# Tiles of a hybrid attention and FFN layer placed at other addresses: the operands of FFN1's up products 64 bytes past their split weights modulo 512, the query, key-value and gate weights 352 bytes further

## The chip, the cores and the metric

The kernel runs on one core of a Trainium2 chip. The metric is the time of one execution in microseconds of device time, the median of several runs. A profiled execution leaves a trace of every instruction on the engines: TensorE (PE, with its weight loads shown apart as PEld), VectorE (DVE), ScalarE (ACT), GpSimd (POOL), and the DMA queue that SyncE (SP) feeds.

## What is computed

One layer over 512 latent tokens and 256 context tokens of width 1024, all in float32: a half-step SwiGLU FFN, token mixing (latent attention with eight heads beside a chunked spatial gate), and a second half-step FFN on the latent tokens.

```python
x = ffn_sublayer(x, mx[0], mx[1], mx[2], norm1_w, ffn1_w1, ffn1_w3, ffn1_w2)
ctx = ffn_sublayer(ctx, mc[0], mc[1], mc[2], norm1_w, ffn1_w1, ffn1_w3, ffn1_w2)
proj = modulate(rms_norm(x, norm2_w), mx[3], mx[4]) @ w_in
...
x = x + mx[5] * token_mix(proj, k_all, v_all, rope, ...)
x = ffn_sublayer(x, mx[6], mx[7], mx[8], norm3_w, ffn2_w1, ffn2_w3, ffn2_w2)
```

with `ffn_sublayer(h) = h + 0.5 * gate * ((silu(n @ w1) * (n @ w3)) @ w2)`, `n` the normed and modulated input. FFN1 works on all 768 tokens, FFN2 on the 512 latent ones; the hidden width is 2816, in 22 blocks of 128.

## The kernel before

Tokens lie along the free dimension, features along the 128 partitions. Every product is made of three matmuls (`mm3`, L165): each operand is kept as a high part in float32r and a low part (the rest), and high by high, low by high and high by low are added up in PSUM. In a name of a matmul the first operand is the moving one, the second the weights: `mm<-hl,oph` streams `hl` past the weights `oph`.

```python
nc.tensor.matmul(out, lh, rh, start=first, stop=False, skip_group_check=more)
nc.tensor.matmul(out, lh, rl, start=False, stop=False, skip_group_check=more)
nc.tensor.matmul(out, ll, rh, start=False, stop=last, skip_group_check=more)
```

Weights come from HBM by SyncE's queue into `raw` or `block` tiles; ScalarE rounds 512 columns to the high part (`oph`) and VectorE subtracts for the low part (`opl`). Five such pairs rotate (`OPS`).

The stages in the order of time:

- First pass of FFN1, to about 61 us: norm and modulation make `hh` and `hl` (L239, L240; 8 blocks of 768 tokens); the first two blocks of the hidden width are done here, with latent tokens 512 wide (`step_mm`) and context tokens 256 wide (`first_ctx`, L573 to L582). The weights of the last three k are split into tiles of the starting pool (`op5` to `op7`).
- FFN1 proper, to about 487 us: two more blocks of the hidden width by plain products, then one level of Winograd's scheme for the up products. Its blocks are four quarters of `hh` and `hl` (L1020) and the token differences `u2`, `u3`, `u4` (L1023), each 384 wide; between them stand down products, whose moving operands `gh`, `gl` are read 256 wide. The order is written out by hand and kept (`Flow`, `Winograd`).
- The last down chunk, 384 wide, to about 538 us. Some of its weights are split into tiles that have come free: `cbl`, `block_l`, `s_l`.
- The input projection (`in_k`, L1292) reads `hh` and `hl` 384 and 256 wide past `oph` and, for the rotary keys, past `kpw` (64 columns). The u and v projection (`uv_unit`, L1364) turns it round: `hh` is the weights, `oph` streams 512 wide. The queries (`q_tile`, L1460) stream `wqh` (L1325) past `cqh` (L1322); the keys and values (`k_mm`, L1526) stream `wkvh` past `ckvh`; the gate (`gate`, L1575) streams `vnh`, which is `mixh` (L1312), past `wsuh`.
- Attention, the output projection (`mixh` past `oph` and `uo`, then `uo` only), and FFN2 (blocks `b11` to `b22`, `t1` to `t4`, 256 wide; `gh`, 512 wide).

Tiles are placed by pools on two stacks, one from the left end of SBUF and one from the right. A pool on the right ends where the one before it begins, so a larger tile under it moves all that come later towards lower addresses. Some small tiles that nobody reads are there only to shift others: `pad_left`, `pad_right` (L237), `pad_mix`, `pad_oap`, `pad_hap` (L1890), `pad_w`, `pad_f2`.

The address of a tile in its partition, modulo 512 bytes, as the pools place it (a step of 128 columns in a weight tile, and one k or one block in a moving tile, is a multiple of 512, so the whole tile has one value):

| tile | role | before | after |
|---|---|---|---|
| `oph`, `opl`, `block_l` | split weights | 448 | 448 |
| `cbl`, `s_l` | split weights of the last down chunk | 384 | 384 |
| `hh`, `hl` | moving; weights in the u and v projection | 448 | 0 |
| `u2`, `u3`, `u4` | moving | 448 | 0 |
| `op5` to `op7` | split weights in the first pass | 448 | 0 |
| `kpw` | weights of the rotary keys, by k | 64, 320 | 128, 384 |
| `gh`, `gl` in FFN1 | moving | 384 | 384 |
| `wqh`, `wql` with `cqh`, `cql` | moving with weights | 96, 96 | 448, 448 |
| `wkvh`, `wkvl` with `ckvh`, `ckvl` | moving with weights | 96, 448 | 448, 448 |
| `mixh` (as `vnh`) with `wsuh` | moving with weights | 448 or 192, 96 | 448 or 192, 448 |
| `mixh`, `mixl` with `uo0`, `uo1` | moving with weights | 448, 384 | 448, 384 |
| `b11`, `b21`, `b22`, `t1` to `t4` (`b12`) | moving in FFN2 | 384 (448) | 384 (448) |
| `w0`, `w1` | split weights at the start of FFN2 | 320 | 320 |

Of the kernel before, what the change touches and what calls it, by code (L numbers as in the profile page):

```python
# [9 lines left out]
F32 = mybir.dt.float32  # L10
# [7 lines left out]
P = 128  # L18
# [155 lines left out]
def layer_kernel(ctx: ExitStack, tc: tile.TileContext, xT, wfirst, wst, wada, wuq, wkpe, cols, wrope, vnw, rope, out):  # L174
# [59 lines left out]

    hctx = ExitStack()
    with right():
        ctx.enter_context(tc.tile_pool(name="pad", bufs=1)).tile([P, 8], F32, name="pad_right")  # L237
        hpool = hctx.enter_context(tc.tile_pool(name="hpool", bufs=1))
    hh = hpool.tile([P, NK, 768], F32R, name="hh")  # L239
    hl = hpool.tile([P, NK, 768], F32R, name="hl")  # L240
# [1067 lines left out]
    p2 = p2ctx.enter_context(tc.tile_pool(name="p2", bufs=1))  # L1308
# [8 lines left out]
    vk = p2.tile([P, 6], F32, name="vk")  # L1317
    rk = p2.tile([P, 6], F32, name="rk")
    sv = p2.tile([P, 6], F32, name="sv")
    p1actx = ExitStack()  # L1320
    p1a = p1actx.enter_context(tc.tile_pool(name="p1a", bufs=1))
    cqh = p1a.tile([P, 2, 512], F32R, name="cqh")  # L1322
# [198 lines left out]
    with right():  # L1521
        kp = kctx.enter_context(tc.tile_pool(name="kpool", bufs=1))
    kn = kp.tile([P, 6, HEADS, QH], F32, name="kn")
    vv = kp.tile([P, 6, HEADS, P], F32R, name="vv")

    def k_mm(t, n, o):  # L1526
        s = slice(t * P, t * P + P)
        m = slice(n * 512, n * 512 + 512)
        mm3(nc, o, (ckvh[:, s], ckvl[:, s]), (wkv[0][:, m], wkv[1][:, m]), True, True)
# [353 lines left out]
    with right():  # L1883
        hap = hactx.enter_context(tc.tile_pool(name="hap", bufs=1))

    def block(pool, name):
        return tuple(pool.tile([P, 4, 256], F32R, bufs=1, name=f"{name}{p}") for p in "hl")

    B11, B21 = block(hap, "b11"), block(hap, "b21")
    hap.tile([P, 16], F32, name="pad_hap")  # L1890
    hbctx = ExitStack()
    with right():
        hbp = hbctx.enter_context(tc.tile_pool(name="hbp", bufs=1))
# [312 lines left out]
```

## Time and profile before

| what | value |
|---|---|
| median of 3 runs | 1112.83 us (1112.6 to 1113.48) |
| span of the profiled execution | 1110.9 us |
| TensorE busy | 1104.4 us, 7616 matmuls |
| weight loads busy | 1056.4 us |
| VectorE, ScalarE, GpSimd busy | 882.9, 537.7, 308.9 us |
| DMA | 125.96 MB, 113 GB/s in the mean |

The profiled execution's own time is given as its span, from the first to the last instruction; the median of the runs is 1.9 us longer, which is what lies around it. A row of the timeline has the start in us, the duration in us, the engine, the line, the operation, the names out<-in, and the shapes. Line L59 is that of a helper through which most instructions pass, so instructions are told apart by their tiles. A matmul's end in the trace is modelled, and rows overlap; the starts are recorded, and the distance from one start to the next is the pace.

### The profile page before, as it was taken

Reading aid. Unit: us, or ns where it says so; the run is one execution under the profiler, and the core shown is the slowest. Engines: PE = TensorE matmul, PEld = TensorE weight load, DVE = VectorE, ACT = ScalarE, POOL = GpSimd, SP = SyncE. Lnnn points to the kernel's source line nnn. Section 1 sums busy time; section 2 is a strip of 40 time slices with the busy share of each in tenths; the row PEclk is TensorE's granted clock in tenths of the full one; section 3 lists DMA queues with packets and bytes.
Section 4 is the critical chain, followed back from the end, with each engine's and each line's share of the span. In section 5 each row is a group of like instructions: output and inputs, shape, how many; then the busy total and the mean of one; then the engine's idle time right before and its main releaser. Section 6 shows DMA issues by size and latency. Waiting matters only on the chain.

```text
span 1110.9 us, 19724 instructions
## 1 busy us (share of the span) xinstructions
PE 1104.4 (99%) x7616; PEld 1056.4 (95%) x7616; DVE 882.9 (79%) x1590; ACT 537.7 (48%) x1110; POOL 308.9 (28%) x268
## 2 busy tenths in 40 slices
PE   9999999999999999999999999999999999999998
PEld 7899999999999999999988889999999989898997
DVE  5779898888888778866756899978886969696884
ACT  6545422431444214444755559985554536353451
POOL 0003303312243023300008427750014425152330
PEclk9999999999999999999999999999999999999999
DMA  9721353344334765312242211003221422333302
GB/s 357 272 65 50 123 169 127 114 135 151 120 107 151 239 200 190 114 59 79 86 134 94 76 38 34 26 21 114 77 96 57 144 86 83 108 115 114 114 2 95
DMA packets 35678, 125.96 MB, mean 113 GB/s; under 512 B 3712, under 2 KB 10624, under 8 KB 30976
## 3 DMA queue, kind: packets, MB, share of 16 engines
q1 hardware_dynamic: 35440, 124.63, 33.1%
q8 instruction: 60, 0.98, 0.4%
q14 instruction: 34, 0.28, 0.1%
q10 hardware_dynamic: 144, 0.06, 0.0%
HBM read 122.58 MB, written 2.10 MB: 112 GB/s over the span
## 4 chain that ended last, share of the span: by engine, by line
PE 94%; DVE 3%; DMA 1%; ACT 1%; issue 0%; POOL 0%; SPq 0%; ACTq 0%; DVEq 0%; POOLq 0%
PE mm L59 55%; PE one L59 19%; PE big L59 8%; PE mm L169 2%; PE mm L170 2%; PE mm L168 2%; PE big L596 1%; PE mm L581 1%; DMA scale<-wada 1%; PE big L170 1%; PE big L168 1%; PE big L169 1%; PE mm L330 1%; DMA x<-xT 0%; DVE opl L59 0%
## 5 line engine op out<-in xcount | busy, mean ns | idle before, releaser
L59 DVE TENSOR_TENSOR opl<-block,oph 128x512 fp32r<-128x512 f32 x216 | 190.0, 888 | 29.8 <-ACT oph L59 27.4
L59 POOL TENSOR_TENSOR block<-block 128x512 f32<-128x512 f32 x69 | 104.1, 1509 | 380.2 <-DVE opl L59 377.6
L59 ACT CAST oph<-block 128x512 fp32r<-128x512 f32 x216 | 133.9, 622 | 109.0 <-PE mm L59 81.9
L59 PE MATMUL mm<-gh,oph 128*128 128x256 f32 (+2 forms) x573 | 176.7, 308 | 0.0
L59 PE MATMUL mm<-gl,oph 128*128 128x256 f32 (+2 forms) x573 | 176.4, 308 | 0.0
L59 PE MATMUL mm<-gh,opl 128*128 128x256 f32 (+2 forms) x573 | 176.4, 308 | 0.0
L59 DVE SCALAR_TENSOR_TENSOR x<-mm,g,x 128x512 f32<-128x512 f32 (+2 forms) x136 | 79.1, 601 | 47.4 <-PE mm L59 47.1
L59 PEld LDWEIGHTS mm<-gl,oph 128*128 128x128 f32 x573 | 107.6, 188 | 5.6
L59 PEld LDWEIGHTS mm<-gh,oph 128*128 128x128 f32 x573 | 107.6, 188 | 5.5
L59 PEld LDWEIGHTS mm<-gh,opl 128*128 128x128 f32 x573 | 107.6, 188 | 5.4
L59 ACT CAST oph<-raw 128x512 fp32r<-128x512 f32 x113 | 68.7, 621 | 77.5 <-PE mm L59 53.0
L59 DVE TENSOR_TENSOR opl<-raw,oph 128x512 fp32r<-128x512 f32 x113 | 77.6, 702 | 11.6 <-ACT oph L59 10.9
L59 POOL TENSOR_TENSOR block<-s,block 128x512 f32<-128x512 f32 x35 | 46.6, 1331 | 130.4 <-DVE opl L59 129.6
L59 PE MATMUL mm<-hh,oph 128*128 128x384 f32 (+2 forms) x195 | 65.2, 334 | 0.0
L59 PE MATMUL mm<-hl,oph 128*128 128x384 f32 (+2 forms) x195 | 64.8, 333 | 0.0
L59 PE MATMUL mm<-hh,opl 128*128 128x384 f32 (+2 forms) x195 | 64.8, 332 | 0.0
L59 DVE SCALAR_TENSOR_TENSOR junk<-raw,cb 128x1024 bf16<-128x1024 f32 x48 | 62.2, 1309 | 0.0
L59 POOL TENSOR_TENSOR s<-block 128x512 f32<-128x512 f32 x34 | 55.6, 1636 | 10.6 <-DMA block<-wst 10.6
L59 DVE SCALAR_TENSOR_TENSOR raw<-raw,cb 128x1024 f32<-128x1024 f32 x32 | 42.2, 1323 | 7.9 <-DMA raw<-wada 7.9
L59 PE MATMUL one<-hl,oph 128*128 128x384 f32 x144 | 48.1, 334 | 0.0
L59 PE MATMUL one<-hh,oph 128*128 128x384 f32 x144 | 48.1, 334 | 0.0
L59 PE MATMUL one<-hh,opl 128*128 128x384 f32 x144 | 48.1, 334 | 0.0
(711 smaller groups left out, 3382.8 us busy)
## 6 DMA issues: line engine op xcount, KB each, us to landing
raw<-wst SPq DMA_DIRECT2D x77, 512.0 KB, 3.9
block<-wst SPq DMA_DIRECT2D x36, 1024.0 KB, 5.0
raw<-wada SPq DMA_DIRECT2D x56, 512.0 KB, 4.3
scale<-wada SPq DMA_DIRECT2D x16, 512.0 KB, 9.0
x<-xT SPq DMA_DIRECT2D x5, 512.0 KB, 6.3
raw<-wfirst SPq DMA_DIRECT2D x8, 256.0 KB, 9.1
out<-x SPq DMA_DIRECT2D x7, 256.0 KB, 2.3
raw<-wuq SPq DMA_DIRECT2D x2, 384.0 KB, 5.1
```

The costliest lines, as they stand in the source:

```text
L59: return lambda *a, **k: self.tc.keep_in_program_order(f(*a, **k))
L168: nc.tensor.matmul(out, lh, rh, start=first, stop=False, skip_group_check=more)
L169: nc.tensor.matmul(out, lh, rl, start=False, stop=False, skip_group_check=more)
L170: nc.tensor.matmul(out, ll, rh, start=False, stop=last, skip_group_check=more)
L330: pin(nc.tensor.matmul(pa[q, :P], scw[:, kt, 2 - 2 * w : 34 - 2 * w], units[d][w][:, kt * P : kt * P + P], start=w == 0 and kt < 4, stop=w ...
L581: pin(nc.tensor.matmul(o, l[:, c], r, start=k == 0 and m == 0 and w == 0, stop=k == NK - 1 and m == 2, skip_group_check=True))
L596: pin(nc.tensor.matmul(two(pbs[i]), ops[k][lo][:, i * P : i * P + P], lat(r, k), start=False, stop=k == NK - 1 and m == 2, skip_group_chec ...
```

## The change

Four pads: `pad_right` grows from 8 to 120 floats, a new `pad_p2` of 88 floats stands behind the small tiles of the token mixing, a new `pad_kp` of 16 floats and `pad_hap`, grown from 16 to 32, together bring the right-hand stack back to where it was modulo 512.

```diff
-        ctx.enter_context(tc.tile_pool(name="pad", bufs=1)).tile([P, 8], F32, name="pad_right")
+        ctx.enter_context(tc.tile_pool(name="pad", bufs=1)).tile([P, 120], F32, name="pad_right")
...
     sv = p2.tile([P, 6], F32, name="sv")
+    p2.tile([P, 88], F32, name="pad_p2")
...
     vv = kp.tile([P, 6, HEADS, P], F32R, name="vv")
+    kp.tile([P, 16], F32, name="pad_kp")
...
-    hap.tile([P, 16], F32, name="pad_hap")
+    hap.tile([P, 32], F32, name="pad_hap")
```

`pad_right` moves `hh`, `hl`, the token differences and the starting pool 448 bytes down, which is 64 up modulo 512. Attention's values `vv` and FFN2's tiles on the right move by 512 in sum. `pad_p2` moves the query weights and their operand, the key-value weights and the gate weights 352 bytes up. No instruction is added or removed: the order on every engine is the same row for row, only addresses differ.

## The prediction

> **What bounds the kernel now.** I read the page first, then the waits of TensorE, then the timeline of TensorE stretch by stretch, because only starts of matmuls tell their real pace. The page:
>
> ```profile
> span 1110.9 us, 19724 instructions
> PE 1104.4 (99%) x7616; PEld 1056.4 (95%) x7616; DVE 882.9 (79%) x1590; ACT 537.7 (48%) x1110; POOL 308.9 (28%) x268
> PE 94%; DVE 3%; DMA 1%; ACT 1%; issue 0%; POOL 0%; SPq 0%; ACTq 0%; DVEq 0%; POOLq 0%
> ```
>
> TensorE is busy 99% of the span and makes up 94% of the chain that ended last. The list of who waited for whom, and the long Winograd stretch of FFN1 as one row of the stretch table (length, then busy time and count of PE, PEld, DVE, ACT, POOL, then the granted clock):
>
> ```profile
> PE mm L288 <- DVE epsc L223: 1.0, 1, 1.0
> 139.00:487.00 348.00, 348.00 (x2414) 348.00 (x2413) 288.65 (x482) 119.84 (x225) 85.32 (x57) 1.00 0.44 146
> ```
>
> TensorE's largest wait of all is 1.0 us, and for 348 us it has no gap at the full clock, with VectorE at 83%. So the time is a sum of matmuls, each by its distance to the next, and a shorter distance is time won. The duration that a row shows is modelled and overlaps the next row; I use distances of starts only. While one matmul streams, the weights of the next are loaded, as these two rows show (both start at 470.93):
>
> ```profile
> 470.93 0.33 PE L59 MATMUL mm<-u4h,opl 128*128 128x384 f32 x1
> 470.93 0.19 PEld L59 LDWEIGHTS mm<-u4h,oph 128*128 128x128 f32 x1
> ```
>
> So the two addresses that can meet are those of the moving operand of one matmul and of the weights of the next. "D" below is the first minus the second, modulo 512 bytes, from the table of addresses above; the change alters D and nothing else, since the order on every engine stays the same.
>
> **What the pace is at each D now.** In each fence stand the first and the last row of a stretch without an interruption. Matmuls 384 columns wide on `hh`, D = 0 (60 from the first to the last):
>
> ```profile
> 472.66 0.33 PE L59 MATMUL mm<-hh,oph 128*128 128x384 f32 x1
> ...
> 483.06 0.33 PE L59 MATMUL one<-u4h,oph 128*128 128x384 f32 x1
> ```
>
> 10.40 us over 60 is 173.3 ns. The same width on `gh` with `oph`, D = -64 (56 apart), and on `gh` with `block_l`, D = -64 too (47 apart):
>
> ```profile
> 487.39 0.34 PE L59 MATMUL mm<-gl,oph 128*128 128x384 f32 x1
> ...
> 497.10 0.34 PE L59 MATMUL mm<-gh,oph 128*128 128x384 f32 x1
> ```
>
> ```profile
> 501.78 0.34 PE L59 MATMUL mm<-gh,block_l 128*128 128x384 f32 x1
> ...
> 510.09 0.33 PE L59 MATMUL mm<-gh,block_l 128*128 128x384 f32 x1
> ```
>
> These are 9.71/56 = 173.4 ns and 8.31/47 = 176.8 ns: 64 bytes apart, the wide matmul is never faster than at D = 0, and in one of the two runs 3.4 ns slower. At 256 columns it is otherwise. D = 0 in the context part of the first pass (92 apart), then D = -64 in FFN1's down products (82 apart):
>
> ```profile
> 49.44 0.28 PE L581 MATMUL mm<-hh,oph 128*128 128x256 f32 x1
> ...
> 60.48 0.28 PE L581 MATMUL mm<-hh,op7l 128*128 128x256 f32 x1
> ```
>
> ```profile
> 140.60 0.28 PE L59 MATMUL mm<-gh,oph 128*128 128x256 f32 x1
> ...
> 149.89 0.28 PE L59 MATMUL mm<-gl,oph 128*128 128x256 f32 x1
> ```
>
> That is 11.04/92 = 120.0 ns against 9.29/82 = 113.3 ns: here D = 0 costs 6.7 ns. And the two stretches with D = +64, the new distance: moving at 448 and weights at 384 (28 apart), then moving at 384 and weights at 320 (47 apart):
>
> ```profile
> 745.96 0.28 PE L59 MATMUL mm<-mixl,uo1h 128*128 128x256 f32 x1
> ...
> 749.13 0.28 PE L59 MATMUL mm<-mixh,uo1l 128*128 128x256 f32 x1
> ```
>
> ```profile
> 766.73 0.28 PE L59 MATMUL big<-b11h,w0h 128*128 128x256 f32 x1
> ...
> 772.26 0.28 PE L59 MATMUL big<-b21h,w1l 128*128 128x256 f32 x1
> ```
>
> 3.17/28 = 113.2 ns and 5.53/47 = 117.7 ns. The same D gives two paces, so D alone does not decide. In the second case the two operands lie in different aligned blocks of 128 bytes, in the first in the same one. The change puts the moving operand at 0 and the weights at 448: different blocks, the second case moved by 128 bytes. For narrow matmuls I therefore take 117.7.
>
> The Trainium skill, "SBUF — State Buffer", section "Who interferes with whom", gives TensorE two independent read ports and says that it never waits on anyone. The trace disagrees at 256 columns (120.0 against 113.3). By that rule the change would be worth exactly nothing, 1112.8 us.
>
> **The change part by part.** How many wide matmuls move: the rows that list the instructions reading one tile, for `hh` and for `u2h`:
>
> ```profile
> L59 PE MATMUL mm<-hh,oph x195: 221/334/632, 60.6 to 562.7; 128*128 128x384 f32 x189, 128*128 128x128 f32 x3, 128*128 128x256 f32 x3
> L59 PE MATMUL one<-hh,oph x144: 334/334/337, 102.2 to 486.7; 128*128 128x384 f32 x144
> L59 PE MATMUL big<-hh,oph x56: 277/334/334, 64.8 to 563.2; 128*128 128x384 f32 x32, 128*128 128x256 f32 x24
> L59 PE MATMUL mm<-u2h,oph x36: 334/334/334, 96.0 to 465.9; 128*128 128x384 f32 x36
> L59 PE MATMUL one<-u2h,oph x36: 334/334/334, 114.8 to 476.3; 128*128 128x384 f32 x36
> ```
>
> Each stands for three products (high by high, low by high, high by low), so `hh` and `hl` are read by 3 x (189 + 144 + 32) = 1095 wide matmuls, and `u2` to `u4` by 3 x 3 x (36 + 36) = 648: 1743 in all, 302 us of the span at 173.3.
>
> 1. *The 1743 wide matmuls, D = 0 to D = +64.* No row shows this width at this D in a steady stretch. Upper bound: the slower D = -64 run, 176.8 - 173.3 = +3.5 ns, 1743 x 3.5 = +6.1 us. Lower bound: the 6.7 ns that narrow matmuls win between D = 0 and D = -64, 1743 x -6.7 = -11.7 us. I take 0, the value of the nearest row in width: the `gh`, `oph` run keeps 173.4 when its operands part by 64 bytes, and the narrow row whose blocks are like the new ones wins only a third of what the best wins. All of it would be on the path; nothing hides it.
> 2. *The first pass's context matmuls* (eight k, four units, three products = 96): 117.7 - 120.0 = -2.3 ns, -0.2 us. Bounds 0 and 96 x -6.7 = -0.6 us.
> 3. *The 96 narrow ones of the input projection* (16 k, two columns of query, three products) stand mixed with wide ones; 0, with the bounds of step 2.
> 4. *The 512-wide latent part of the first pass* waits for its operands anyway:
>
> ```profile
>   ACT hh L59: 11.5, 24
> ```
>
> TensorE was idle 11.5 us for `hh`, mostly there. A few ns in a matmul change when it begins to wait, not when the next `hh` arrives: 0, hidden by ScalarE. Without that cover the some 80 matmuls at the 6.7 ns of step 1 would be 0.5 us either way.
>
> 5. *The key-value products*, 512 wide and 352 bytes on, come from D = 160 to D = 0. Before (6 apart):
>
> ```profile
> 621.32 0.40 PE L59 MATMUL big<-wkvh,ckvh 128*128 128x512 f32 x1
> ...
> 622.72 0.28 PE L59 MATMUL mm<-mixh,wsuh 128*128 128x256 f32 x1
> ```
>
> 1.40/6 = 233.3 ns. At D = 0 the step from 256 to 384 columns added 173.3 - 120.0 = 53.3 ns, so 512 columns at D = 0 would take 226.7 (an estimate): 36 x -6.6 = -0.2 us. Bounds 0 and twice that.
>
> 6. *Query products* keep D = 0, since both operands move by 352: 0. *The 24 gate products* come to D = 0 and D = 256; at the 6.7 ns of step 1 they are 0.2 us at most, either way; I take 0.
> 7. *The u and v projection* reads `hh` as weights: 192 matmuls 512 wide go from D = 0 to D = -64. Bounds +6.6 (the key-value row's excess) and -6.7 ns: +1.3 and -1.3 us; I take 0 by the row of step 1 that kept its pace.
> 8. *FFN2, attention and the output projection* keep every D: the right-hand tiles there move by 512 in sum. The pads hold no work. 0.
>
> Sum: -0.2 - 0.2 = -0.4 us on a span of 1110.9, so 1110.5. The profiled execution shows its span alone; the median 1112.83 is 1.9 us longer, which I keep: 1112.4.
>
> **The rivals.**
>
> *Slower: the wide matmul settles at the slower pace.* Place: FFN1's up products and Winograd products, 61 to 487 us, and the projection. For it: the `block_l` run at 176.8 through 47 matmuls without one relief, and the narrow `w` row, whose operands lie in different blocks as the new ones will, is 4.5 ns worse than the best. Against: the `oph` run with its 173.4. Price: 1743 x 3.5 = +6.1 us, 1118.5; with the bound of step 7, 1119.8. It decides from 0.43 of the wide matmuls on (2.6 us of 6.1, the 0.4 of gain made up).
>
> *Faster: the wide matmul sheds what the narrow one sheds.* For it: at D = 0, 128 columns cost 53.3 ns (step 5), so 256 would cost 106.7 and both widths carry the same 13.3 ns on top (120.0 - 106.7 and 173.3 - 160.0); of that constant 6.7 ns went away at 256 columns. The `mixh` row shows that +64 can shed it too. Against: the two `gh` rows, which shed none at 384. Price -11.7 us, so 1112.4 - 11.7 = 1100.7. VectorE has the room: 288.65 us of 348 become 86% if the stretch shrinks by 10 us. It decides from 1.0 ns a matmul on (1.8 us).
>
> The Trainium skill, "TensorE: Matmul & The Clock Gate", section "Back-to-back issue gap", puts the isolated gap at N / 2.4 + 2.5 ns, an estimate of 162.5 ns for 384 columns; the trace's 173.3 is 10.8 longer, so by that page there is room for this rival, and 1743 x 10.8 would be 18.8 us. No run here shows that pace.
>
> *The change does not do what it says for the clock at all:* the distance does not matter at this width and the narrow ones gain nothing either: 1112.8. It falls into the range of the forecast.
>
> **How the numbers follow.** A measurement of this kernel can tell about 0.2%, 2.2 us, from no change. The forecast, with its own range 1109.9 to 1114.1 (steps 2, 3, 5 and 7 all at their bounds): 0.45. Faster rival, in full or in part: 0.28. Slower rival, in full or in part: 0.27. No rival can be left out with 0.2, so the range reaches to both: 1100.5 to 1119.8. Faster by over 0.2%: 0.28; within: 0.45; slower: 0.27.
>
> **What would show it right or wrong.** In the profile of the changed kernel the distance of wide `hh` and `u` starts between 139 and 487 us: 173.3 for the forecast, about 176.8 for the slower, below 172 for the faster rival. Step 2: 92 matmuls of L581 in 10.83 us. Step 5: six key-value products in 1.36 us. Step 8: `gh` with `oph` at 113.3 and FFN2 as before. Wrong would be a change of pace in a stretch whose D stays, or a new wait of TensorE.

## The result and the profile after

The changed kernel takes 1118.45 us (median of 4 runs, 1118.08 to 1118.64) against 1112.71 (4 runs beside it, 1112.46 to 1113.48): a ratio of 1.0049, 95% interval 1.0037 to 1.0062. It is 5.7 us slower; 1112.4 was forecast, with a range of 1100.5 to 1119.8. The time is that of the slower rival (1118.5), but not by its mechanism.

The page of after:

```profile
span 1116.3 us, 19724 instructions
PE 1109.6 (99%) x7616; PEld 1061.2 (95%) x7616; DVE 881.8 (79%) x1590; ACT 537.1 (48%) x1110; POOL 310.0 (28%) x268
```

The span is 5.4 us longer and TensorE is busy 5.2 us longer, with the same count of instructions; the other engines are where they were, within 1.1 us. The longest waits of TensorE are those of before:

```profile
PE mm L288 <- DVE epsc L223: 1.0, 1, 1.0
PE mm L59 <- DVE u L59: 1.0, 3, 0.4
PE big L588 <- ACT hh L59: 0.4, 1, 0.4
```

So no wait was added: matmuls follow each other at a longer distance. Which ones, the timeline tells. The matmuls that were moved in FFN1, 384 wide on `hh`, first and last of 61 without an interruption:

```profile
473.87 0.34 PE L59 MATMUL one<-hh,oph 128*128 128x384 f32 x1
...
484.27 0.34 PE L59 MATMUL one<-hh,oph 128*128 128x384 f32 x1
```

10.40 us over 60 is 173.3 ns, to the digit the pace of before. The matmuls that were *not* moved, FFN1's down products, `gh` past `oph` at D = -64 (82 from the first to the last, as in the prediction's fence):

```profile
140.80 0.28 PE L59 MATMUL mm<-gh,oph 128*128 128x256 f32 x1
...
150.46 0.28 PE L59 MATMUL mm<-gl,oph 128*128 128x256 f32 x1
```

9.66 us over 82 is 117.8 ns; before it was 113.3. It stays so for whole chunks. Here is the third chunk from its first to its last matmul (431 apart), of before and then of after:

```profile
367.51 0.28 PE L59 MATMUL mm<-gh,oph 128*128 128x256 f32 x1
...
416.38 0.28 PE L59 MATMUL mm<-gh,opl 128*128 128x256 f32 x1
```

```profile
370.48 0.28 PE L59 MATMUL mm<-gh,oph 128*128 128x256 f32 x1
...
421.23 0.28 PE L59 MATMUL mm<-gh,opl 128*128 128x256 f32 x1
```

48.87 us became 50.75. The other two chunks (359 apart each) went from 40.71 to 42.28 us, so the three together from 130.29 to 135.31: +5.02 us of the 5.4. The table of groups marks it too. The loads of the three kinds of products, in before and in after (busy time, then mean ns of one):

```profile
L59 PEld LDWEIGHTS mm<-gl,oph 128*128 128x128 f32 x573 | 107.6, 188 | 5.6
L59 PEld LDWEIGHTS mm<-gh,oph 128*128 128x128 f32 x573 | 107.6, 188 | 5.5
L59 PEld LDWEIGHTS mm<-gh,opl 128*128 128x128 f32 x573 | 107.6, 188 | 5.4
```

```profile
L59 PEld LDWEIGHTS mm<-gh,opl 128*128 128x128 f32 x573 | 109.2, 191 | 5.5
L59 PEld LDWEIGHTS mm<-gh,oph 128*128 128x128 f32 x573 | 107.6, 188 | 5.6
L59 PEld LDWEIGHTS mm<-gl,oph 128*128 128x128 f32 x573 | 107.6, 188 | 5.6
```

In the slow chunks one load of every three takes longer, that of `mm<-gh,opl` (192 ns for every one between 141 and 182 us in after, the other two kinds 187 to 188); in the fast pace all three are alike.

The rest of the difference is the u and v projection, 512 wide with `hh` as weights. One of its units in before and the same unit in after (23 apart):

```profile
589.79 0.40 PE L168 MATMUL mm<-oph,hh 128*128 128x512 f32 x1
...
595.05 0.40 PE L170 MATMUL mm<-oph,hl 128*128 128x512 f32 x1
```

```profile
594.69 0.39 PE L168 MATMUL mm<-oph,hh 128*128 128x512 f32 x1
...
600.06 0.40 PE L170 MATMUL mm<-oph,hl 128*128 128x512 f32 x1
```

5.26/23 = 228.7 against 5.37/23 = 233.5 ns. From start to start its 192 matmuls take 44.58 us in before and 45.41 in after, +0.83. Against that stand -0.14 us in the first pass (11.04 to 10.90 us for the 92 matmuls of the prediction's fence):

```profile
49.46 0.28 PE L581 MATMUL mm<-hh,oph 128*128 128x256 f32 x1
...
60.36 0.28 PE L581 MATMUL mm<-hh,op7l 128*128 128x256 f32 x1
```

and smaller sums of both signs.

The trace of before already held the key, in a stretch that the prediction did not read. In FFN2, `b` and `t` blocks stream past `oph` at D = -64 without a change of address. Pieces of TensorE's timeline in before, with a short stall between the rows at 863.32 and 863.50:

```profile
850.29 0.28 PE L59 MATMUL one<-t3h,opl 128*128 128x256 f32 x1
...
863.21 0.28 PE L59 MATMUL mm<-t4h,opl 128*128 128x256 f32 x1
863.32 0.34 PE L59 MATMUL mm<-b22h,oph 128*128 128x256 f32 x1
863.50 0.28 PE L59 MATMUL mm<-b22l,oph 128*128 128x256 f32 x1
...
873.15 0.28 PE L59 MATMUL one<-t4h,opl 128*128 128x256 f32 x1
873.37 0.38 PE L59 MATMUL one<-b22h,oph 128*128 128x256 f32 x1
873.59 0.28 PE L59 MATMUL one<-b22l,oph 128*128 128x256 f32 x1
...
874.29 0.28 PE L59 MATMUL one<-b22l,oph 128*128 128x256 f32 x1
...
875.99 0.28 PE L59 MATMUL mm<-t1l,oph 128*128 128x256 f32 x1
```

Up to 863.21 it is 12.92/114 = 113.3 ns. At 863.32 the next start is 0.18 us away instead of 0.11. From 863.50 to 873.15 it is 9.65/82 = 117.7 ns, with the same tiles. Then come two long steps (starts at 873.15, 873.37 and 873.59), and from 874.29 on it is 1.70/15 = 113.3 again. One distance, one width, two paces, and the change from one to the other comes where steps are 60 to 110 ns longer than the pace. Not every stall brings a change: at the same place of later blocks, steps of 0.55 and 0.22 us (from 882.90 on) leave the pace at 113.3, and steps of 0.57 and 0.22 us (from 1004.55 on) are followed by steps of 117 to 118 ns.

### The profile page after: what moved, and what is told of

The parts are those of the page before. It is cut to its first block, busy times and chain, and to the rows that moved or that the text cites. A ratio compares the mean times of both kernels' runs of the same rounds, so it can differ in the third digit from the quotient of the medians.

```text
span 1116.3 us, 19724 instructions
## 1 busy us (share of the span) xinstructions
PE 1109.6 (99%) x7616; PEld 1061.2 (95%) x7616; DVE 881.8 (79%) x1590; ACT 537.1 (48%) x1110; POOL 310.0 (28%) x268
## 4 chain that ended last, share of the span: by engine, by line
PE 93%; DVE 4%; ACT 1%; DMA 1%; issue 1%; POOL 0%; SPq 0%; DVEq 0%; ACTq 0%; POOLq 0%
PE mm L59 55%; PE one L59 19%; PE big L59 8%; PE mm L170 2%; PE mm L169 2%; PE mm L168 2%; PE big L596 1%; PE mm L581 1%; DMA scale<-wada 1%; DVE opl L59 1%; PE big L170 1%; PE big L168 1%; PE big L169 1%; PE mm L330 1%; DMA x<-xT 0%
## 5 line engine op out<-in xcount | busy, mean ns | idle before, releaser
L59 PEld LDWEIGHTS mm<-gl,oph 128*128 128x128 f32 x573 | 107.6, 188 | 5.6
L59 PEld LDWEIGHTS mm<-gh,oph 128*128 128x128 f32 x573 | 107.6, 188 | 5.6
```

The source lines that it names most:

```text
L59: return lambda *a, **k: self.tc.keep_in_program_order(f(*a, **k))
```

## The theories

*Entry:* 256-wide matmuls at D = -64 have two steady paces (modes), 113.3 and 117.8 ns, with the same addresses. Which one holds is carried from matmul to matmul; it is set where the run is entered, by the matmuls in front or by a stall. The change altered only the `hh` matmuls in front of the down products, and through them the mode.

*Address (the rival):* the place of `hh` acts on the down products directly, for instance through whoever else reads or writes there; then the pace goes with the place of `hh`, whatever stands in front.

## The experiments

Each run stands beside the kernel before on the same chip (medians 1112.77, 1113.23 and 1112.84 us in three sets). Paces are those of the first chunk of down products.

| run | place of `hh` | what precedes the down products | pace, ns | time, us | ratio (95%) |
|---|---|---|---|---|---|
| before | 448 | `hh` 128, then 256 wide | 113.3 | 1112.71 | |
| after | 0 | the same | 117.8 | 1118.45 | 1.0049 (1.0037 to 1.0062) |
| right_only | 0 | the same | 117.8 | 1118.17 | 1.0047 (1.0034 to 1.0059) |
| p2_only | 448 | the same | 113.3 | 1112.53 | 0.9997 (0.9988 to 1.0006) |
| before_nocut | 448 | `hh` 384 wide | 113.3 | 1112.12 | 0.9993 (0.9984 to 1.0003) |
| after_nocut | 0 | `hh` 384 wide | 117.8 | 1117.68 | 1.0043 (1.0028 to 1.0058) |
| after_rev | 0 | `hh` 256, then 128 wide | 113.3 | 1113.02 | 0.9999 (0.9989 to 1.0008) |
| before_rev | 448 | `hh` 256, then 128 wide | 113.3 | 1112.87 | 1.0000 (0.9991 to 1.0009) |
| after_kick6 | 0 | six matmuls at D = 0 | 113.3 | 1115.08 | 1.0018 (1.0008 to 1.0028) |
| after_split | 0 | cut inside the run | 117.8, 117.8 behind the cut | 1118.97 | 1.0052 (1.0037 to 1.0067) |
| before_split | 448 | cut inside the run | 113.3, 113.3 behind the cut | 1113.78 | 1.0007 (0.9998 to 1.0016) |
| hh384 | 384 | `hh` 128, then 256 wide | 113.3 | 1113.55 | 1.0002 (0.9993 to 1.0012) |
| hh256 | 256 | the same | 117.8 | 1118.00 | 1.0044 (1.0028 to 1.0059) |
| best | 448 | `hh` 384 wide | 113.3 | 1111.86 | 0.9988 (0.9980 to 0.9997) |

**Which half of the change.** `right_only` is the change without `pad_p2`:

```diff
-    p2.tile([P, 88], F32, name="pad_p2")
```

> The right-hand part alone (hh, hl and the u tiles at 0 instead of 448 modulo 512), without the pad in front of the query and key-value weights. If the loss comes from the place of hh, as the entry theory (the hh matmuls in front put the down products of FFN1 into a slower pace) and the address theory (the place of hh acts on the down products directly) both say: +5.0 to +5.5 us for the 1152 down products of the three chunks at 117.8 instead of 113.4 ns, +0.8 us for the u and v projection, -0.2 us in the first pass, so about 1118.5 us. If the loss needs the pad of the query and key-value weights: no more than 1113.5.

`p2_only` is the kernel before with that one line added.

> The pad of 352 bytes in front of the query and key-value weights alone, hh where it was. Both theories: the down products stay at 113.4 ns; 36 key-value products lose at most 6 ns each, so -0.2 us or less and 1112.5 us, not to be told from no change. A result above 1114 us would speak against both.

1118.17 and 1112.53: the whole loss is in the right-hand part. Between before and `right_only` the down products differ by +5.03 us and the u and v projection by +0.81; no other stage by more than some 0.2 (the input projection, -0.21). The 36 key-value products take 8.55 us in before, 8.39 in `p2_only`, and 8.52 in after.

**Another entry, first try.** The same edit in the kernel before (`before_nocut`) and the changed one (`after_nocut`):

```diff
-            self.product(banks[2], "B22", False, ev_hi(seeded), cut=n > 256 and f in DOWN1)
+            self.product(banks[2], "B22", False, ev_hi(seeded), cut=False)
```

> The kernel before, in which the last product of hh ahead of the down products is no longer cut into a part of 128 and one of 256 columns, so that the down products follow matmuls of 384 columns. No address changes. Entry theory: the pace of a whole chunk hangs on what stands in front, so the down products may now run at 117.8 ns from the first to the last: up to 1152 x 4.4 ns = +5.1 us, about 1117.5 us; if this entry happens to lead to the fast pace too, 113.4 ns and about 1112.5 us. Address theory: 113.4 ns whatever stands in front, 1112.5 us, give or take 0.5 us for the cut itself.

> The same edit on the changed kernel: the down products follow matmuls of 384 columns on hh at 0. Entry theory: the down products may run at 113.4 ns, which gives back some 5 us (about 1113.5 us); if this entry too leads to the slow pace, 117.8 ns and about 1118.5 us. Address theory: 117.8 ns whatever stands in front, about 1118.5 us. This run and the one before it together tell the theories apart as soon as one of the two changes its pace.

Neither changed its pace: 113.3 and 117.8 ns. The two runs tell nothing apart. They show that the cut is not what makes the difference, and that without it the medians of both kernels are 0.6 to 0.8 us shorter, which for the kernel before still lies within the interval of no change.

**Another entry, second try.** `after_rev` is the changed kernel with the two parts of the cut product in the other order; `before_rev` is its control.

```diff
-            parts = ((256, n), (0, 256)) if cut and i == 3 else ((0, n),)
+            parts = ((0, 256), (256, n)) if cut and i == 3 else ((0, n),)
...
-                    i == 3 and a == 0, not first)
+                    i == 3 and b == n, not first)
```

> The changed kernel with the two parts of the cut product in the other order, so that the down products follow three matmuls of 128 columns on hh and not three of 256. Entry theory: again a new entry, 113.4 ns (about 1113.5 us) or 117.8 ns (about 1118.4 us), the same in all three chunks since they are entered alike. Address theory: 117.8 ns, 1118.4 us.

> The kernel before with the two parts of the cut product in the other order, the control for the run that gave 5.4 us back on the changed kernel. Entry theory: a new entry for the down products; 113.4 ns if it leads to the fast pace as on the changed kernel (about 1112.6 us, so the order itself costs next to nothing and the 5.4 us there were the pace), or 117.8 ns (about 1117.7 us). If the order of the parts were worth 5 us by itself (an eviction that comes free sooner), this run would be near 1107.5 us.

`after_rev` gives the whole loss of the down products back: 1113.02. The timeline of `after_rev` around the first chunk, up to the chunk's last matmul:

```profile
139.50 0.22 PE L59 MATMUL mm<-hh,oph 128*128 128x128 f32 x1
...
139.67 0.28 PE L59 MATMUL mm<-hh,opl 128*128 128x128 f32 x1
139.78 0.33 PE L59 MATMUL mm<-gh,oph 128*128 128x256 f32 x1
139.95 0.28 PE L59 MATMUL mm<-gl,oph 128*128 128x256 f32 x1
...
180.53 0.28 PE L59 MATMUL mm<-gh,opl 128*128 128x256 f32 x1
```

From 139.95 on it is 40.58/358 = 113.4 ns. Every tile is where it is in after, the matmuls are the same in number and size, only the six of the cut product ahead of each chunk stand in another order. With them the step of 0.17 us behind the three short matmuls moves and now lies on the first down product (139.78 to 139.95); the run does not tell the order of the six from this step. The loads of weights are alike again (107.6 us in all three groups). The control, 1112.87, shows that the order by itself is worth nothing. So the address theory falls: with `hh` at 0 the down products run at either pace, as their entry has it.

**A push in front.** Six matmuls at D = 0 ahead of each chunk of the changed kernel; what they write is overwritten by the products that follow.

```diff
             pts = [mm(), mm()]
+            for _ in range(6 if dt == 0 else 0):
+                nc.tensor.matmul(pts[0][:, 0:256], pairs[0][0][:, 0:P], pairs[0][0][:, 0:256], start=True, stop=True)
```

> The changed kernel with six extra matmuls of 256 columns ahead of each of the three chunks of down products, at distance 0 (split weights against split weights); their output is overwritten. No address changes. Entry theory: in the trace of before, six such matmuls at 120 ns in front of a run at distance -64 led it to 113.3 ns every time in FFN2 (after 121, 122, 115, 115), so the down products run at 113.4 again: -1152 x 4.4 ns = -5.1 us, plus 18 x 120 ns = +2.2 us, so 1118.4 - 2.9 = 1115.5 us. Address theory: 117.8 ns as in the changed kernel, plus the 2.2 us, so 1120.6 us.

1115.08 against 1115.5 expected. In this trace the row of the six and what follows:

```profile
139.43 0.89 PE L59 MATMUL mm<-oph 128*128 128x256 f32 x6
140.15 0.29 PE L59 MATMUL mm<-gh,oph 128*128 128x256 f32 x1
140.27 0.28 PE L59 MATMUL mm<-gl,oph 128*128 128x256 f32 x1
140.40 0.28 PE L59 MATMUL mm<-gh,opl 128*128 128x256 f32 x1
...
141.08 0.28 PE L59 MATMUL mm<-gh,opl 128*128 128x256 f32 x1
...
150.37 0.28 PE L59 MATMUL mm<-gh,oph 128*128 128x256 f32 x1
```

Two slower steps (0.12, 0.13), and from 141.08 on 9.29/82 = 113.3 ns. 18 added matmuls make the kernel 3.4 us shorter than the changed one, though on a chip where the kernel before took 0.5 us longer.

It is not a rule that matmuls at D = 0 lead to the fast pace. In the trace of before, `b21` streams past `t3` and `t4` (both at 384, so D = 0) and is followed by `b11` and `b21` past `oph` (D = -64):

```profile
777.08 0.28 PE L59 MATMUL mm<-b21h,t3l 128*128 128x256 f32 x1
...
779.00 0.28 PE L59 MATMUL big<-b11h,oph 128*128 128x256 f32 x1
...
784.30 0.28 PE L59 MATMUL big<-b21h,oph 128*128 128x256 f32 x1
```

1.92/16 = 120.0 ns, and behind it 5.30/45 = 117.8: the slow pace. So "every time in FFN2" in the expectation holds for the six matmuls that it counted, not for every run entered from D = 0.

**Is the mode carried?** The same cut in the middle of a run, in the changed kernel (`after_split`) and in the kernel before (`before_split`): three matmuls of 256 columns become six of 128.

```diff
-                    mm3(nc, o, [a[:, u * P : u * P + P] for a in pairs[q]], g, fi == 0, fi == n - 1)
+                    ws = [a[:, u * P : u * P + P] for a in pairs[q]]
+                    for c in (0, 128) if (dt, t, fi) == (2, 1, 1) else (None,):
+                        s = slice(c, None if c is None else c + 128)
+                        mm3(nc, o if c is None else o[:, s], ws, g if c is None else [a[:, s] for a in g], fi == 0, fi == n - 1)
```

> The changed kernel, in which one product of each chunk of down products (third column block, middle third, second unit) is cut into two halves of 128 columns: six short matmuls in place of three, in the middle of the run. Entry theory: the short matmuls are a new entry for the rest of the run, so it may leave 117.8 for 113.3 ns (up to 0.7 of 1152 x 4.4 ns = -3.5 us, about 1115.2 us with 0.3 us for the short matmuls), or come back to 117.8 (about 1118.7 us). Address theory: 117.8 ns on both sides of the cut, 1118.7 us.

> The kernel before with one product of each chunk of down products cut into two halves of 128 columns, the mirror of the same cut in the changed kernel. There the rest of the run came out of the short matmuls with 117.8 ns, as it went in. Entry theory, form 1 (the short matmuls alone set what follows): the rest runs at 117.8 here too, 0.7 x 1152 x 4.4 ns = +3.5 us and 0.5 us for the cut, about 1116.7 us. Form 2 (the mode is carried through the short matmuls): 113.4 on both sides, only the cut's 0.5 us, about 1113.2 us. In both forms the addresses of these matmuls are those of the changed kernel to the byte.

`after_split`, the last of the six, the entry behind them, and 82 steps of what follows:

```profile
152.81 0.27 PE L59 MATMUL mm<-gh,opl 128*128 128x128 f32 x1
152.91 0.33 PE L59 MATMUL mm<-gh,oph 128*128 128x256 f32 x1
...
153.20 0.28 PE L59 MATMUL mm<-gh,opl 128*128 128x256 f32 x1
...
162.86 0.28 PE L59 MATMUL mm<-gh,oph 128*128 128x256 f32 x1
```

`before_split`, the same place:

```profile
152.57 0.28 PE L59 MATMUL mm<-gh,opl 128*128 128x128 f32 x1
152.69 0.33 PE L59 MATMUL mm<-gh,oph 128*128 128x256 f32 x1
...
153.44 0.28 PE L59 MATMUL mm<-gh,oph 128*128 128x256 f32 x1
...
162.73 0.28 PE L59 MATMUL mm<-gl,oph 128*128 128x256 f32 x1
```

9.66/82 = 117.8 and 9.29/82 = 113.3 ns. Around the cut the two kernels run the same matmuls at the same addresses for some 100 matmuls in front of it and 249 behind it, and still each keeps its own pace. This is form 2 of the expectation: the mode is carried through the six short matmuls. The cost of the cut itself was set too low, 1113.78 instead of 1113.2.

**Other places for `hh`.** `hh384` has `pad_right` at 24 floats and `hh256` at 56, with `pad_kp` and `pad_hap` making up 512 bytes. The edit for `hh384`:

```diff
-        ctx.enter_context(tc.tile_pool(name="pad", bufs=1)).tile([P, 8], F32, name="pad_right")
+        ctx.enter_context(tc.tile_pool(name="pad", bufs=1)).tile([P, 24], F32, name="pad_right")
...
+    kp.tile([P, 112], F32, name="pad_kp")
...
-    hap.tile([P, 16], F32, name="pad_hap")
+    hap.tile([P, 128], F32, name="pad_hap")
```

> hh, hl and the u tiles at 384 modulo 512, 64 bytes before the split weights instead of 64 past them: distance -64, that of the down products. Entry theory: the 1743 wide matmuls take one of the paces that gh shows at this distance (173.3, 174.6 or 176.7 ns): 0 to +6.0 us by the pace of their mode; the down products take over the mode they are entered with, 113.4 or 117.8 ns: 1112.5 to 1118 us in the first case, up to 1124 us with both. Address theory: distance -64 is what gh has itself, and the products of hh cost as in the changed kernel or less: no prediction for the down products beyond 117.8 where hh is away from 448. The u and v projection at distance +64 (512 wide): if every distance but 0 costs 233 instead of 227 ns, +0.8 us as in the changed kernel.

> hh, hl and the u tiles at 256 modulo 512, distance -192. If the wide matmul keeps 173.3 ns at distances of 0, +64 and -64 because the distance does not matter at that width: 173.3 again. If only distances of less than 128 bytes are that good: up to 176.7 ns, +5.9 us. The u and v projection, 512 wide at distance +192: 227 ns if it is the sign of the distance, 233 ns if every distance but 0 costs that (+0.8 us). Down products 113.4 or 117.8 ns by their entry: 1112.5 to 1113.5 us, or 1118 us.

Wide `hh` matmuls in `hh256`, at D = -192 (60 apart), then in `hh384`, at D = -64 (60 apart):

```profile
473.73 0.34 PE L59 MATMUL one<-hh,oph 128*128 128x384 f32 x1
...
484.13 0.34 PE L59 MATMUL one<-hh,oph 128*128 128x384 f32 x1
```

```profile
468.42 0.34 PE L59 MATMUL one<-hh,oph 128*128 128x384 f32 x1
...
478.82 0.34 PE L59 MATMUL one<-hh,oph 128*128 128x384 f32 x1
```

10.40 us over 60 in both: 173.3 ns at -192, -64, 0 and +64. The down products come out at 117.8 ns with `hh` at 0 and 256 and at 113.3 with `hh` at 384 and 448. The u and v projection differs from before by +0.81 us in `hh256` (D = +192) and +0.22 in `hh384` (D = +64), so not every distance other than 0 costs the +0.8 that was expected for that case.

The narrow `hh` matmuls do follow its place. The first pass's context matmuls past `oph` are the same instructions in every run; from 50 us on they follow each other at 120.0 ns in before (D = 0), 117.8 in after (+64), 117.8 in `hh256` (-192) and 113.3 in `hh384` (-64). In the last three runs the down products have the same pace as these. This fits a mode that is handed on from matmul to matmul, but it is not a test of its own.

**Both small gains together.** `best` is the kernel before with `pad_p2` of 88 floats and `cut=False`.

> The kernel before with the pad of 352 bytes in front of the query and key-value weights and without the cut of the last hh product: the two edits that alone came out 0.24 and 0.65 us below the kernel before. Both theories: down products at 113.3 ns as in each of the two, so the sum, 1111.9 us, at the edge of what can be told from the kernel before. If the two do not add, 1112.1 to 1112.8.

1111.86 us, as expected: 0.9988 of the kernel before, with an interval that just leaves out 1. It is the fastest of all.

## Why the prediction was wrong

- *What bounds the kernel* was right: TensorE without gaps, the time a sum of distances between starts. The sentence that failed is "the change alters D and nothing else", together with what the sum took from it: where D stays, the pace stays. D is not all that a pace depends on. The prediction had two pieces of evidence in its own rows: 173.4 and 176.8 ns for `gh` at one and the same D, and 113.2 and 117.7 ns at D = +64. It noted that "D alone does not decide" and then sought the missing part in the address (aligned blocks of 128 bytes). For `gh` at D = -64 and 256 columns the runs show that it is in what came before; for the two pairs of rows themselves nothing was tried.
- *Step 1* was right: 1743 matmuls, 173.3 ns as before, 0. `hh256` and `hh384` show why both rivals failed. The steady pace of the wide `hh` matmuls does not follow the place of `hh` (the most that the 1743 lost anywhere is 0.6 us in `hh384`), so there was neither a gain of 11.7 us to be had nor a loss of 6.1.
- *Step 2* had the right sign and the right pace, and a wrong count: `op5` to `op7` move together with `hh`, so 36 of its 96 matmuls keep D = 0. In after those past `op6` and `op7` still take 120.0 ns and those past `oph` 117.8 from 50 us on; in sum 10.90/92 = 118.5 ns, -0.14 us instead of -0.2. *Step 3* stayed at nothing as taken: all 225 matmuls 256 wide on `hh` and `hl`, those of step 2 among them, became 0.2 us shorter in sum. *Step 4* came out at nothing (84 matmuls, 21.14 us before and 21.18 after), but its reason misread the row: of the 11.5 us, 10.1 are idle time of VectorE, which waits for `hh` to write `hl`. TensorE itself waited for `hh` once, 0.4 us, as its list of waits shows.
- *Step 5* failed in size: 8.55 to 8.52 us for the 36, not -0.2; with `pad_p2` alone it is -0.16. The estimate of 226.7 ns at D = 0 was right for a steady step (226 to 227 ns in 24 of the 36 in `p2_only`), but the first dozen in after take 224 to 236, or wait. *Step 6*: right, within 0.1 us each.
- *Step 7* was taken at 0 and came out at +0.83, inside its bounds of 1.3. The key-value row's 233.3 ns was the nearer row; the value was taken from a run of another width.
- *Step 8* is where it failed. It puts stretches that "keep every D" at 0, and for the stretches that it lists this held (FFN2 and the output projection within 0.1 us each). But FFN1's down products have no term in the sum at all; the prediction names them only under step 8 of its signs, "`gh` with `oph` at 113.3 and FFN2 as before". They cost +5.02 us, 117.8 for 113.3 ns, in 1152 matmuls whose addresses do not change. The prediction named this case as what would prove it wrong ("a change of pace in a stretch whose D stays") but gave it no price. A price was there to be had: two paces 4.4 ns apart at 256 columns, 1152 such matmuls in the three chunks, 5.1 us, as a rival of its own.
- *The slower rival* had the right time by luck: its 1118.5 comes from moved wide matmuls at 176.8 ns, and these stayed at 173.3.

The Trainium skill, "TensorE: Matmul & The Clock Gate", section "Back-to-back issue gap", says that in a stream of weight loads and matmuls the spacing is set by both, pipelined. The traces agree in so far as the slow pace comes with one longer load in three (a mean of 191 ns in its group against 188).

## What to carry to other kernels

Where TensorE is the bound and has no gaps, read the pace of each stretch from starts, and look for one and the same kind of matmul with two paces in one trace: if there is one, the pace may hang on how the stretch was entered, and then any edit in front of it, a moved tile, another order, a stall, can gain or lose the difference over the whole stretch. So price such a switch as a rival (difference of the paces times the matmuls behind the edit), and when a kernel turns slower after a change that cannot have cost anything, compare paces where nothing was changed first. Before giving up an edit, try another order of the last few matmuls ahead of the stretch: here that was worth 5.4 us and cost nothing.

## What the runs showed of the hardware

- 256-wide float32r matmuls at D = -64 have two steady paces, 113.3 and 117.8 ns, each held over 430 matmuls and more, with the same addresses. The mode survived six matmuls of 128 columns. It changed with six matmuls at D = 0 in front, with another order of `hh` matmuls in front, and at some stalls; other stalls left it, and another run at D = 0 led to the slow pace.
- The slow pace has a mark in the table of groups: of three kinds of weight loads, one has a busy time 1.6 us above the other two (192 ns for one load in the slow chunks, against 188).
- 384-wide matmuls on `hh` run at 173.3 ns at D = 0, +64, -64 and -192. The 256-wide ones of the first pass past `oph` run at 120.0, 117.8, 113.3 and 117.8 ns there.
- What the mode is, inside the engine, stays open, and so does the rule by which an entry chooses it: `hh` at 448 and 384 led to the fast pace, at 0 and 256 to the slow one, and with the parts in the other order 0 led to the fast one too. Whether the u and v projection's +0.8 us (`hh` at 0 and 256) is a price of the distance or such a mode was not tried.
